# Late weight loads on another queue, sums of the first gate group on VectorE, another PSUM bank, and another order from the scheduler in a hybrid FoX/RWKV-7 layer

## The chip, the cores and the metric

The kernel runs on one core of a Trainium2 chip. The metric is device time in microseconds of one execution. Engines are named as the profile names them: PE is TensorE (matmuls; PEld its weight loads), DVE is VectorE, ACT is ScalarE, POOL is GpSimd, and SP (SPq in a timeline) is SyncE, which here only issues DMAs.

## What is computed

T = 512 tokens of width 2048 go through one layer with two branches. In outline:

```
h = rmsnorm(x) * norm_gain;  u = h @ w_in;  split u -> u_fox, u_rwkv, g_a, g_b
o_a = causal attention with forget gates over q, k, v (8 heads of 128) * silu(z_a)
r, kr, vr, z_b, w_down, a_down = token_shift(u_rwkv)          # 16 heads of 64
decay = exp(-exp(w));  a = sigmoid(a0 + a_down @ a2);  kk = kr*k_k / max(|kr*k_k|, eps)
S = S*decay + (S @ -kk) (kk*a)^T + v k^T;  y = S r           # for every token
o_b = (groupnorm(y) + bonus) * silu(z_b)
m = sigmoid(g_a) * (o_a @ w_proj_fox) + sigmoid(g_b) * (o_b @ w_proj_rwkv)
out = final_rmsnorm(x + m @ w_out)
```

## The kernel before

All products are done in float32 accuracy: each operand is split into a high and a low part, and a product is three matmuls (high by high, high by low, low by high). A weight piece is loaded by SP as `raw_*`, ACT writes its high part `whi_*` (line 267) and DVE its low part `wlo_*` (line 268).

The first stage runs 16 units in turn: `rw0`, `fox0`, ..., `rw7`, `fox7`. A unit is a list of weight products (`u_*`); between their matmuls PE does the small work of the scan and of the attention heads. The scan is done for pairs of heads (p = 0 to 7) in chunks of 64 tokens (c = 0 to 7). Each pair has a front (`rwkv_front`: the norm `kn`, root on ACT at line 537, TENSOR_SCALAR at 538 and four RECIPROCALs at 541 on DVE; the decays `tz`, lines 520 to 523; then `E1`, `EK`, `AR`, `rkk`, `rhi`/`rlo`), a back (`rwkv_back`: `BK` and the matrices of the chunks), and a chain (`rwkv_chain`, lines 696 to 774). The chain goes through the chunks one after the other. For chunk c: the matmul `z` gives a PSUM tile, whose two halves are copied to `zt` by DVE (line 717) and ACT (718); the matmul `sa` reads `zt`, and its result is copied to `AV` by DVE (727) and ACT (728); the matmul `st` reads `AV`; two DVE operations make the next state `SV` from it (735), which the next chunk's `z` reads. In the time of pair p's chain, PE also runs the front of pair p+1.

The order of PE and of SP is the order of the program text, which a planner with fixed lags (`LAG`) interleaves from the workers. The orders of DVE, ACT and POOL are set by the framework's scheduler from what is ready and from priorities: the chain's operations, for one, are written under a high priority (`HP`).

Then come the gates. Stage `c` (lines 1071 to 1102, the columns of one quarter for each group g = 0 to 3) uses weight pieces `g{g}_{kb}_{k}`; its two PSUM tiles `c11_g_0` and `c11_g_1` are of the kind `ps_mm` (two banks), which the units before it use too: `fz` at line 848 reads the last of them. While it runs, DVE makes the sums `d1`, `s3`, `s2` and `s4` of quarters of the activations (`sum_step`). The other quarters are computed by `gates_rest` with fewer products, from sums of weight blocks: for each group units "5" (block 11 + 12), "7" (12 + 22), "6", "3" and "4", each of four steps j of 12 matmuls with weights of 128x1024, whose parts `h` and `l` ACT and DVE split from `X` or `b`. For the first group (g = 0), `X` is loaded, block 12 is added onto it by an accumulating DMA, and so are later 22 (line 994) and 21 (998). These DMAs are issued by POOL for the first four units, and later plain loads by SP. The first group's units 5 and 7 alternate over j, then come the four steps of 6. `open_late` (938) opens the pool of `gates_rest` as soon as all chains have ended. After the gates follow the two projections (`p`) and the output product (`o`), whose first weights are `raw_p0_0_0` to `_3`.

Of the kernel before, what the change touches and what calls it, by code (L numbers as in the profile page):

```python
# [9 lines left out]
F32 = mybir.dt.float32  # L10
F32R = mybir.dt.float32r
AF = mybir.ActivationFunctionType
ALU = mybir.AluOpType
# [4 lines left out]
P = 128  # L18
# [24 lines left out]
HP = 300  # L43
# [13 lines left out]
def hybrid_layer(  # L57
# [6 lines left out]
    nc = tc.nc  # L64
    V, S, G, PE = nc.vector, nc.scalar, nc.gpsimd, nc.tensor
# [76 lines left out]
    def ps_mm(name):  # L142
        return psm.tile([P, T], F32, tag="mm", bufs=2, name=name)

    def ps_ms(name):
        return psm.tile([P, T], F32, tag="ms", bufs=3, name=name)
# [146 lines left out]
    def u_tile(name):  # L293
        ps = ps_mm(f"u_{name}")
        yield from product(ps, name, lambda k: hhi[:, k, :], lambda k: hlo[:, k, :])
        return ps
# [18 lines left out]
    def gate_w(g, kb, cb, j, n=2):  # L315

        c0 = (GB0 if g < 2 else GA0) + g % 2 * 1024 + cb * 512
        r0 = (kb * KB + j * n) * P
        return w_in[r0:r0 + n * P, c0:c0 + 512]
# [24 lines left out]
    for hf in range(2):  # L344
        t = slice(256 * hf, 256 * hf + 256)
# [75 lines left out]
    def split(hi, lo, a):  # L421

        S.copy(hi, a)  # L423
        V.tensor_tensor(lo, a, hi.bitcast(F32), ALU.subtract)  # L424
# [55 lines left out]
    p1_d = dram.tile([4, 2, P, T], F32, name="p1_d")  # L480

    def tt(eng, o, a, b, op=ALU.mult):
        eng.tensor_tensor(o, a, b, op)  # L483
# [375 lines left out]
    def stage1():  # L859
        ps = yield from u_tile("ad")  # L860
# [5 lines left out]
        for kind, i in units:  # L866
            if kind == "rw":
                for nm, blk in (("k", 1), ("r", 0), ("z", 3), ("v", 2)):
                    ps = yield from u_tile(f"{nm}{i}")
# [68 lines left out]
        def open_late():  # L938

            if not opened and chain.done:  # L940
                rw_stack.close()
                opened.append(late_stack.enter_context(tc.tile_pool(name="gw", bufs=1, reuse_waits="tile")))
                rest.append(gates_rest(opened[0]))
                next(rest[0])


        def gates_rest(wp):
# [5 lines left out]
            raw, xs, ready = {}, {}, {}  # L953
            at = [0]

            def load(upto):
                while at[0] < len(loads) and loads[at[0]][0] <= upto:
                    n, b = loads[at[0]]
                    at[0] += 1
                    g, p, j = units[n]  # L960
                    onto = g == 0 and b == "11"
                    if onto:
                        t = xs[j] = wp.tile([P, 2, 512], F32, tag="X", bufs=4, name=f"X_{g}{j}")
                    else:
                        t = wp.tile([P, 2, 512], F32, tag=f"b{b}", bufs=3 if b == "22" else 2, name=f"b{b}_{g}{p}{j}")

                    with tc.high_priority(offset=HP if n < 4 else 0):
                        (G if n < 4 else nc.sync).dma_start(t, rows(g, b, j))
                        if onto:
                            G.dma_start(t, rows(g, "12", j), accum_op=ALU.add)  # L970
                    raw[n, b] = t

            def rows(g, b, j):
                return gate_w(g, int(b[0]) - 1, int(b[1]) - 1, j).rearrange("(k p) m -> p k m", p=P)

            def prep(n):
                g, p, j = units[n]
                if p == "5" and g == 0:
                    src = xs[j]
                elif p == "5":  # L980
                    src = xs[j] = wp.tile([P, 2, 512], F32, tag="X", bufs=4, name=f"X_{g}{j}")
                    tt(V, src, raw[n, "11"], raw[n, "12"], ALU.add)
                elif p == "7":
                    src = raw[n - 1, "12"]
                    tt(V, src, src, raw[n, "22"], ALU.add)
                else:
                    src = raw[n, "22"] if p == "3" else xs[j]
                hi = wp.tile([P, 2, 512], F32R, tag="hi", bufs=3, name=f"h{g}{p}{j}")
                lo = wp.tile([P, 2, 512], F32R, tag="lo", bufs=3, name=f"l{g}{p}{j}")
                split(hi, lo, src)  # L990
                ready[n] = (hi, lo)
                if p == "7":
                    if g == 0:
                        G.dma_start(xs[j], rows(g, "22", j), accum_op=ALU.add)
                    else:
                        tt(V, xs[j], xs[j], raw[n, "22"], ALU.add)
                elif p == "6":
                    G.dma_start(xs[j], rows(g, "21", j), accum_op=ALU.add)

# [5 lines left out]
                    done.append(m)  # L1005

            done = []
            load(1)
            ready_upto(1)
            yield  # L1010
            left = [("s4", j) for j in range(4)]
            ev = lambda tag, nm: wp.tile([P, T], F32, tag=tag, bufs=4 if tag == "p1" else 2, name=nm)
            for n, (g, p, j) in enumerate(units):
                ready_upto(n + 2)
                load(n + 4)
                if (p, j) == ("5", 0):
                    pz = [ps_mm(f"z5_{g}_{t}") for t in range(2)]
                    p1 = [ev("p1", f"p1_{g}_{t}") for t in range(2)]
                    for t in range(2):
                        (G if g == 0 else nc.sync).dma_start(p1[t], p1_d[g, t])  # L1020
                elif (p, j) == ("7", 0):
                    if g % 2:
                        px = [ps_ms(f"x7_{g}"), ps_y(f"y7_{g}")]
                    else:
                        px = [psm.tile([P, T], F32, tag="ch", bufs=2, name=f"x7_{g}_{t}") for t in range(2)]
                elif (p, j) == ("6", 0):
                    py = [ps_ms(f"y6_{g}_{t}") for t in range(2)]
                ps = pz if p in "53" else px if p in "74" else py
                hi, lo = ready.pop(n)
                begin, end = p in "576", p in "634"  # L1030
                for t in range(2):
                    for kk in range(2):
                        k = 2 * j + kk
                        th, kb = {"7": (1, 0), "6": (0, 0), "3": (0, 1), "4": (1, 1)}.get(p, (0, 0))
                        if p == "5":
                            ah, al = (a[:, kk, t * P:(t + 1) * P] for a in d1[j])
                        else:
                            ts = slice(256 * th + t * P, 256 * th + (t + 1) * P)
                            ah, al = (a[:, KB * kb + k, ts] for a in (hhi, hlo))
                        for a, w, i in ((ah, hi, 0), (ah, lo, 1), (al, hi, 2)):  # L1040
                            mm(ps[t], a, w[:, kk, :], start=begin and k == 0 and i == 0,
                               stop=end and k == KB - 1 and i == 2, skip_group_check=True)
                            yield
                    if j < 3:
                        continue
                    if p == "5":
                        p5 = [None, None] if t == 0 else p5
                        p5[t] = ev("p5", f"p5_{g}_{t}")
                        S.copy(p5[t], ps[t])
                    elif p == "6":  # L1050
                        tt(V, p1[t], p1[t], py[t], ALU.add)
                        u3 = ev("u3", f"u3_{g}_{t}")
                        tt(V, u3, p1[t], px[t], ALU.add)
                        tt(V, p5[t], p5[t], u3, ALU.subtract)
                        S.activation(p5[t], p5[t], AF.Tanh, scale=0.5)
                        store_gate(p5[t], g, 1, 1, t)
                    elif p == "3":
                        u3 = ev("u3", f"c12_{g}_{t}")
                        tt(V, u3, pz[t], p1[t], ALU.subtract)
                        S.activation(u3, u3, AF.Tanh, scale=0.5)  # L1060
                        store_gate(u3, g, 0, 1, t)
                    elif p == "4":
                        tt(V, p1[t], p1[t], px[t], ALU.add)
                        S.activation(p1[t], p1[t], AF.Tanh, scale=0.5)
                        store_gate(p1[t], g, 1, 0, t)
                if g == 3 and p in "34" and j % 2 == 0:
                    split_o(len(o_first), 0, ob_d)
                if left and p == "6":
                    sum_step(*left.pop(0))

        rest = []
        for g in range(4):
            ps = [ps_mm(f"c11_{g}_{t}") for t in range(2)]
            for kb in range(2):
                for j in range(4):
                    ws = [next_piece(), next_piece()]
# [3 lines left out]
                    for kk, t in order:  # L1080
# [7 lines left out]
                        if j == 3 and kk == 1:  # L1088
                            if kb == 0:
                                p1 = keep.tile([P, T], F32, tag=KEEP[t], name=f"p1_{g}_{t}")  # L1090
# [9 lines left out]
                        sum_step(*first_sums.pop(0))  # L1100
                    if g == 3 and kb == 1 and not first_sums:
                        sum_step("s2", j)
                    open_late()
        if first_sums or len(d1) < 4:
            raise ValueError("the sums come too late")
        while not opened:
# [96 lines left out]
    for tb in range(4):  # L1203
        t = fin.tile([P, D], F32, tag="xo", bufs=4, name=f"xo_{tb}")
# [98 lines left out]
```

## Time and profile before

| | us |
|---|---|
| median of 3 runs | 1668.12 (1667.06 to 1669.88) |
| the profiled execution | 1671.53 |
| its span in the profile | 1669.8 |
| PE busy | 1603.4 |
| DVE busy | 1118.0 |
| ACT busy | 770.0 |
| POOL busy | 118.3 |

The durations used below come from the one profiled execution. Its time is 3.4 us above the median. Idle time of PE is the span less PE's busy time; the list of waits says for what it was idle, and a timeline gives each instruction's start, its duration and, in brackets, the idle time ahead of it with what ended that.

### The profile page before, as it was taken

The numbers are of one execution on the slowest core, as the hardware profiler recorded it, in microseconds if no ns is written. First come the engines' busy times: TensorE is split into PE (matmuls) and PEld (weight loads), VectorE is DVE, ScalarE is ACT, GpSimd is POOL, SyncE is SP. The second block draws the span as 40 slices with busy tenths as digits, with TensorE's granted clock in tenths as the row PEclk, the third lists the DMA queues.
The fourth block names the chain that finished last, engine by engine and source line by source line (L and its number), as shares of the span: only waits on it lengthen the run. The fifth ranks groups of instructions, "written<-read, shape, count | busy, mean of one in ns | idle before, by whom it ended". The sixth has DMA issues, their size and how long they took to land. (4 is left out here: it accounts for less than half of the span.)

```text
span 1669.8 us, 23495 instructions
## 1 busy us (share of the span) xinstructions
PE 1603.4 (96%) x8378; PEld 1302.3 (78%) x8378; DVE 1118.0 (67%) x2165; ACT 770.0 (46%) x1503; POOL 118.3 (7%) x181
## 2 busy tenths in 40 slices
PE   6999999999999999999999899599999999999998
PEld 6888787787887877877878677478888788888886
DVE  6467777786687777776876779677877335444432
ACT  7533645536446445464464376344445223323322
POOL 3010000000001000001000000311000000001110
PEclk9999999999999999999999999799999999999999
DMA  5343334243333342433333466997776545563422
GB/s 167 98 105 90 84 86 106 61 120 86 86 93 96 90 106 70 111 87 86 90 98 92 117 190 197 261 279 191 237 236 174 163 153 164 158 202 132 139 82 101
DMA packets 239595, 220.58 MB, mean 132 GB/s; under 512 B 40454, under 2 KB 174190, under 8 KB 238838
## 3 DMA queue, kind: packets, MB, share of 16 engines
q1 hardware_dynamic: 222662, 179.73, 38.3%
q0 software_dynamic: 9616, 25.72, 6.6%
q10 hardware_dynamic: 7200, 13.63, 2.2%
q8 instruction: 66, 1.08, 0.3%
q14 instruction: 51, 0.42, 0.1%
HBM read 198.04 MB, written 20.99 MB: 131 GB/s over the span
## 5 line engine op out<-in xcount | busy, mean ns | idle before, releaser
L136 PE MATMUL p<-whi_p,o 128*128 128x512 f32 x512 | 164.3, 398 | 2.3 <-ACT whi_p L267 2.3
L136 PEld LDWEIGHTS p<-whi_p,o 128*128 128x128 f32 x512 | 97.0, 190 | 24.4 <-ACT whi_p L267 2.7
L483 DVE TENSOR_TENSOR Wt<-W,Lt 128x16 f32<-128x16 f32 (+30 forms) x248 | 101.6, 410 | 6.5
L268 DVE TENSOR_TENSOR wlo_p<-raw_p,whi_p 128x512 fp32r<-128x512 f32 x64 | 43.5, 691 | 91.9 <-ACT whi_p L267 91.9
L136 PE MATMUL p<-wlo_p,o 128*128 128x512 f32 x256 | 101.4, 396 | 0.3 <-DVE wlo_p L268 0.2
L267 ACT ACTIVATE whi_p<-raw_p 128x512 fp32r<-128x512 f32 x64 | 40.4, 632 | 119.0 <-PE p L136 47.4
L268 DVE TENSOR_TENSOR wlo_o<-raw_o,whi_o 128x512 fp32r<-128x512 f32 x56 | 42.3, 761 | 69.8 <-ACT whi_o L267 69.5
L136 PE MATMUL o<-whi_o,mhi 128*128 128x512 f32 x224 | 87.6, 391 | 0.0
L136 PE MATMUL o<-whi_o,mlo 128*128 128x512 f32 x224 | 87.2, 389 | 0.0
L136 PE MATMUL o<-wlo_o,mhi 128*128 128x512 f32 x224 | 87.1, 389 | 0.0
L423 ACT CAST h<-X 128x1024 fp32r<-128x1024 f32 x48 | 50.1, 1051 | 79.4 <-DMA X<-in_w_in_dram 22.7
L424 DVE TENSOR_TENSOR l<-X,h 128x1024 fp32r<-128x1024 f32 x48 | 58.4, 1223 | 31.9 <-ACT h L423 31.9
L643 DVE TENSOR_REDUCE W<-Wt 128x8 f32<-128x16 f32 (+30 forms) x248 | 72.7, 293 | 5.7
L267 ACT ACTIVATE whi_o<-raw_o 128x512 fp32r<-128x512 f32 x56 | 35.2, 631 | 78.5 <-PE o L136 70.8
L136 PE MATMUL c<-whi_g,hhi 128*128 128x512 f32 x128 | 52.4, 409 | 7.2 <-DVE fz L848 4.5
L136 PEld LDWEIGHTS p<-wlo_p,o 128*128 128x128 f32 x256 | 48.4, 189 | 11.6 <-DVE wlo_p L268 1.0
L722 ACT ACTIVATE pre<-SV,E 64x64 f32<-64x64 f32 x112 | 38.6, 345 | 39.7 <-DVE SV L735 38.4
L267 ACT ACTIVATE whi_g<-raw_g 128x512 fp32r<-128x512 f32 x64 | 39.9, 630 | 31.6 <-PE c L136 14.3
L268 DVE TENSOR_TENSOR wlo_g<-raw_g,whi_g 128x512 fp32r<-128x512 f32 x64 | 43.2, 686 | 14.2 <-ACT whi_g L267 13.5
L136 PE MATMUL u_fq<-hhi,whi_fq 128*128 128x512 f32 x128 | 52.5, 410 | 0.0
L136 PE MATMUL u_fq<-hlo,whi_fq 128*128 128x512 f32 x128 | 52.4, 409 | 0.0
L136 PE MATMUL c<-wlo_g,hhi 128*128 128x512 f32 x128 | 52.0, 406 | 0.2 <-DVE wlo_g L268 0.2
(428 smaller groups left out, 4671.6 us busy)
## 6 DMA issues: line engine op xcount, KB each, us to landing
b<-in_w_in_dram SPq DMA_DIRECT2D x56, 512.0 KB
raw_g<-in_w_in_dram SPq DMA_DIRECT2D x64, 256.0 KB
raw_o<-in_w_out_dram SPq DMA_DIRECT2D x56, 256.0 KB
X<-in_w_in_dram POOLq DMA_DIRECT2D x26, 512.0 KB, 7.1
raw_k<-in_w_in_dram SPq DMA_DIRECT2D x32, 256.0 KB
raw_r<-in_w_in_dram SPq DMA_DIRECT2D x32, 256.0 KB
raw_z<-in_w_in_dram SPq DMA_DIRECT2D x32, 256.0 KB
raw_v<-in_w_in_dram SPq DMA_DIRECT2D x32, 256.0 KB
```

Of the source, the lines that this page charges most:

```text
L136: PE.matmul(out, lhsT=lhsT, rhs=rhs, start=start, stop=stop, **kw)
L267: S.activation(whi, raw, AF.Copy)
L268: V.tensor_tensor(wlo, raw, whi.bitcast(F32), ALU.subtract)
L423: S.copy(hi, a)
L424: V.tensor_tensor(lo, a, hi.bitcast(F32), ALU.subtract)
L483: eng.tensor_tensor(o, a, b, op)
L643: V.tensor_reduce(W[:, :, i], tmp[:, :, 0:i + 1], AX.X, ALU.add)
L722: S.activation(pre[hs[q]], SV[hs[q], c, q, :], AF.Copy, scale=E1[hs[q], c, CH:CH + 1])
```

## The change

Five things are changed. (1) For g = 0 the blocks 11, 12 and 22 are plain loads by SP like those of the other groups, and DVE adds them: `X` = b11 + b12, and `X` += b22 behind unit 7. (2) The tiles `p1` of g = 0 are loaded by SP, too. (3) The second tile of the first group's `c` sum is in the bank of `ps_y`. (4) `open_late` is called in the last step of `c` only. (5) The framework's scheduler sets the orders of DVE, ACT and POOL by a time line of its own. The orders of PE and SP are as before but for the loads named; on DVE 1409 of 2165 instructions, on ACT 532 of 1499 stand at another place, and POOL has 16 DMAs fewer.

```diff
                     g, p, j = units[n]
-                    onto = g == 0 and b == "11"
-                    if onto:
-                        t = xs[j] = wp.tile([P, 2, 512], F32, tag="X", bufs=4, name=f"X_{g}{j}")
-                    else:
-                        t = wp.tile([P, 2, 512], F32, tag=f"b{b}", bufs=3 if b == "22" else 2, name=f"b{b}_{g}{p}{j}")
-
-                    with tc.high_priority(offset=HP if n < 4 else 0):
-                        (G if n < 4 else nc.sync).dma_start(t, rows(g, b, j))
-                        if onto:
-                            G.dma_start(t, rows(g, "12", j), accum_op=ALU.add)
+                    t = wp.tile([P, 2, 512], F32, tag=f"b{b}", bufs=3 if b == "22" else 2, name=f"b{b}_{g}{p}{j}")
+                    nc.sync.dma_start(t, rows(g, b, j))
...
-                if p == "5" and g == 0:
-                    src = xs[j]
-                elif p == "5":
+                if p == "5":
...
                 if p == "7":
-                    if g == 0:
-                        G.dma_start(xs[j], rows(g, "22", j), accum_op=ALU.add)
-                    else:
-                        tt(V, xs[j], xs[j], raw[n, "22"], ALU.add)
+                    tt(V, xs[j], xs[j], raw[n, "22"], ALU.add)
...
-            load(1)
...
-                        (G if g == 0 else nc.sync).dma_start(p1[t], p1_d[g, t])
+                        nc.sync.dma_start(p1[t], p1_d[g, t])
...
-            ps = [ps_mm(f"c11_{g}_{t}") for t in range(2)]
+            ps = [ps_mm(f"c11_{g}_0"), (ps_mm if g else ps_y)(f"c11_{g}_1")]
...
-                    open_late()
+                    if g == 3 and kb == 1 and j == 3:
+                        open_late()
...
-    with _tile.TileContext(nc) as tc:
+    with _tile.TileContext(nc, schedule_with_timeline_sim=True) as tc:
```

The first place is DVE in chain 2, chunks 1 and 2, where the front of pair 3 is done. In a name the first number is the pair (`_2_`, `_3`), the second the chunk; `kn_3` is the norm of pair 3. Before:

```order
L717 COPY zt_2_4111<-z_2_1_4109 64x64
L727 COPY AV_2_4017<-sa_2_1_4161 64x64
L538 TENSOR_SCALAR kn_3_4143<-kn_3_4143 128x512
L541 RECIPROCAL kn_3_4143<-kn_3_4143 128x128 x2
L735 SCALAR_TENSOR_TENSOR SV_2_3271<-st_2_1_4172,E1_0_483,pre_2_4114 64x64 x2
L268 TENSOR_TENSOR wlo_v3_8_4211<-raw_v3_8_4102,whi_v3_8_4210 128x512
L521 TENSOR_SCALAR tz_3_4127<-tz_3_4127 128x512
L541 RECIPROCAL kn_3_4143<-kn_3_4143 128x128
L717 COPY zt_2_4194<-z_2_2_4192 64x64
L522 SCALAR_TENSOR_TENSOR tz_3_4127<-reset_531,tz_3_4127 128x512
L268 TENSOR_TENSOR wlo_v3_12_4246<-raw_v3_12_4177,whi_v3_12_4245 128x512
L447 SCALAR_TENSOR_TENSOR z_3_4203<-u_z3_4029,par1m_452,z_3_4203 128x511
```

After, from the same `zt` of chunk 1 on:

```order
L717 COPY zt_2_4111<-z_2_1_4109 64x64
L268 TENSOR_TENSOR wlo_v3_4_4180<-raw_v3_4_4080,whi_v3_4_4179 128x512
L538 TENSOR_SCALAR kn_3_4143<-kn_3_4143 128x512
L541 RECIPROCAL kn_3_4143<-kn_3_4143 128x128 x4
L521 TENSOR_SCALAR tz_3_4127<-tz_3_4127 128x512
L727 COPY AV_2_4017<-sa_2_1_4161 64x64
L483 TENSOR_TENSOR EK_3_4132<-EK_3_4132,k_3_3859 128x512
L543 SCALAR_TENSOR_TENSOR kn_3_4143<-k_3_3859,par_448,kn_3_4143 128x512
L522 SCALAR_TENSOR_TENSOR tz_3_4127<-reset_531,tz_3_4127 128x512
L551 SCALAR_TENSOR_TENSOR rkk_3_4155<-r_3_4025,par_448,EK_3_4132 128x512
L735 SCALAR_TENSOR_TENSOR SV_2_3271<-st_2_1_4172,E1_0_483,pre_2_4114 64x64 x2
```

and further, to the copy of chunk 2's `AV`:

```order
L268 TENSOR_TENSOR wlo_v3_8_4211<-raw_v3_8_4102,whi_v3_8_4210 128x512
L546 SCALAR_TENSOR_TENSOR AR_3_4151<-kn_3_4143,E1_1_484 128x8x64
L483 TENSOR_TENSOR AR_3_4151<-r_3_4025,E1_1_484 128x8x64
L483 TENSOR_TENSOR BK_3_4324<-EK_3_4132 64x8x64 x2
L717 COPY zt_2_4194<-z_2_2_4192 64x64
L268 TENSOR_TENSOR wlo_v3_12_4246<-raw_v3_12_4177,whi_v3_12_4245 128x512
L447 SCALAR_TENSOR_TENSOR z_3_4203<-u_z3_4029,par1m_452,z_3_4203 128x511
L424 TENSOR_TENSOR rlo_3_4158<-rkk_3_4155,rhi_3_4157 128x512
L483 TENSOR_TENSOR BK_3_4324<-kn_3_4143,EK_3_4132 64x8x64 x2
L727 COPY AV_2_4017<-sa_2_2_4218 64x64
```

The copy `AV_2` from `sa_2_1` stood ahead of the front's first operation and now stands behind six of them (one TENSOR_SCALAR, four RECIPROCALs and the TENSOR_SCALAR of `tz`); the rest of the front, which was spread up to chunk 3, now stands between `AV` of chunk 1 and `AV` of chunk 2.

The second place is DVE in chain 3, chunks 0 and 1, with the front of pair 4. Before:

```order
L727 COPY AV_3_5208<-sa_3_0_5239 64x64
L268 TENSOR_TENSOR wlo_v4_4_5318<-raw_v4_4_5214,whi_v4_4_5317 128x512
L735 SCALAR_TENSOR_TENSOR SV_3_4387<-st_3_0_5293,E1_1_484,pre_3_5229 64x64 x2
L538 TENSOR_SCALAR kn_4_5275<-kn_4_5275 128x512
L541 RECIPROCAL kn_4_5275<-kn_4_5275 128x128 x2
L717 COPY zt_3_5309<-z_3_1_5307 64x64
L521 TENSOR_SCALAR tz_4_5259<-tz_4_5259 128x512
L541 RECIPROCAL kn_4_5275<-kn_4_5275 128x128
L268 TENSOR_TENSOR wlo_v4_8_5345<-raw_v4_8_5244,whi_v4_8_5344 128x512
L727 COPY AV_3_5208<-sa_3_1_5328 64x64
L522 SCALAR_TENSOR_TENSOR tz_4_5259<-reset_531,tz_4_5259 128x512
L483 TENSOR_TENSOR EK_4_5264<-EK_4_5264,k_4_4990 128x512
```

After:

```order
L727 COPY AV_3_5208<-sa_3_0_5239 64x64
L268 TENSOR_TENSOR wlo_v4_4_5318<-raw_v4_4_5214,whi_v4_4_5317 128x512
L538 TENSOR_SCALAR kn_4_5275<-kn_4_5275 128x512
L541 RECIPROCAL kn_4_5275<-kn_4_5275 128x128 x4
L521 TENSOR_SCALAR tz_4_5259<-tz_4_5259 128x512
L735 SCALAR_TENSOR_TENSOR SV_3_4387<-st_3_0_5293,E1_1_484,pre_3_5229 64x64 x2
L483 TENSOR_TENSOR EK_4_5264<-EK_4_5264,k_4_4990 128x512
L268 TENSOR_TENSOR wlo_v4_8_5345<-raw_v4_8_5244,whi_v4_8_5344 128x512
L543 SCALAR_TENSOR_TENSOR kn_4_5275<-k_4_4990,par_448,kn_4_5275 128x512
L522 SCALAR_TENSOR_TENSOR tz_4_5259<-reset_531,tz_4_5259 128x512
L717 COPY zt_3_5309<-z_3_1_5307 64x64
L551 SCALAR_TENSOR_TENSOR rkk_4_5287<-r_4_5147,par_448,EK_4_5264 128x512
```

Here it is the state `SV_3` of chunk 0 that stood ahead of `kn_4` and now stands behind the TENSOR_SCALAR, the four RECIPROCALs and that of `tz_4`.

The third place is SP's queue behind the first pieces of the projection (`raw_p0`), with the loads of `gates_rest` (b11, b12, b22 of group 0; the last digit is j). Before:

```order
L240 DMA raw_p0_0_3_10713<-in_w_proj_rwkv_dram 128x512
L968 DMA X_02_10755<-in_w_in_dram 128x2x512
L968 DMA b12_052_10758<-in_w_in_dram 128x2x512
L968 DMA b22_072_10784<-in_w_in_dram 128x2x512
L968 DMA X_03_10804<-in_w_in_dram 128x2x512
L968 DMA b12_053_10807<-in_w_in_dram 128x2x512
L968 DMA b22_073_10827<-in_w_in_dram 128x2x512
```

After:

```order
L240 DMA raw_p0_0_3_10692<-in_w_proj_rwkv_dram 128x512
L962 DMA b11_050_10727<-in_w_in_dram 128x2x512
L962 DMA b12_050_10729<-in_w_in_dram 128x2x512
L962 DMA b22_070_10737<-in_w_in_dram 128x2x512
L962 DMA b11_051_10745<-in_w_in_dram 128x2x512
L962 DMA b12_051_10747<-in_w_in_dram 128x2x512
L962 DMA b22_071_10755<-in_w_in_dram 128x2x512
L962 DMA b11_052_10757<-in_w_in_dram 128x2x512
L962 DMA b12_052_10759<-in_w_in_dram 128x2x512
L1006 DMA p1_0_0_10763<-p1_d_561 128x512
L1006 DMA p1_0_1_10764<-p1_d_561 128x512
L962 DMA b22_072_10785<-in_w_in_dram 128x2x512
```

SP got the ten loads that POOL had issued; they stand behind `raw_p0_0_3` as SP's first late load did. On DVE, the split of the first unit now follows a sum of two loads:

```order
L483 TENSOR_TENSOR X_00_10731<-b11_050_10727,b12_050_10729 128x1024
L483 TENSOR_TENSOR st_s4_1_10964<-hhi_99 128x512
L424 TENSOR_TENSOR hlo_100<-st_s4_0_10938,hhi_99 128x2x256
L483 TENSOR_TENSOR b12_050_10729<-b12_050_10729,b22_070_10737 128x1024
L424 TENSOR_TENSOR l050_10734<-X_00_10731,h050_10733 128x1024
L483 TENSOR_TENSOR su_s4_1_10965<-hlo_100 128x512
L483 TENSOR_TENSOR X_01_10749<-b11_051_10745,b12_051_10747 128x1024
L424 TENSOR_TENSOR l070_10741<-b12_050_10729,h070_10740 128x1024
L483 TENSOR_TENSOR X_00_10731<-X_00_10731,b22_070_10737 128x1024
```

Eight such sums are new on DVE: four of b11 and b12, and four that add b22 to `X`. Before, `X` came ready from the accumulating DMA.

## Rows read from the trace of the kernel before

**Rows 1.** The page: span, then part 1, busy time and share of each engine.
```profile
span 1669.8 us, 23495 instructions
...
PE 1603.4 (96%) x8378; PEld 1302.3 (78%) x8378; DVE 1118.0 (67%) x2165; ACT 770.0 (46%) x1503; POOL 118.3 (7%) x181
```

**Rows 2.** PE's waits: line waited for, total us, times, longest.
```profile
PE z L136 <- ACT h L423: 18.5, 3, 14.4
...
PE c L136 <- DVE fz L848: 4.5, 1, 4.5
```

**Rows 3.** Timeline of PE at the end of c: start, us, line, names, idle.
```profile
1063.98 0.79 PE L136 MATMUL z<-h,d_fqh 128*128 128x512 f32 x1 [14.38 <-ACT h L423]
```

**Rows 4.** Chain of work that ended last: start us, us, what.
```profile
1100.15 10.99 PE y L136 x48
```

**Rows 5.** Windows: stretch, us, busy time of each engine, clock, DMA.
```profile
45.00:950.00 905.00, 888.10 (x5077) 720.47 (x5075) 674.89 (x1518) 452.66 (x975) 46.55 (x61) 1.00 0.37 93
```

**Rows 6.** Timeline of DVE, chain 2 with the front of pair 3.
```profile
407.27 0.22 DVE L727 COPY AV<-sa 64x64 f32<-64x64 f32 x1 [1.68 <-PE sa L136]
407.77 0.43 DVE L538 TENSOR_SCALAR kn<-kn 128x512 f32<-128x512 f32 x1 [0.28 <-ACT kn L537]
408.24 1.76 DVE L541 RECIPROCAL kn<-kn 128x128 f32<-128x128 f32 x2
409.92 0.48 DVE L735 SCALAR_TENSOR_TENSOR SV<-st,E,pre 64x64 f32<-64x64 f32 x2
410.53 0.69 DVE L268 TENSOR_TENSOR wlo_v<-raw_v,whi_v 128x512 fp32r<-128x512 f32 x1
411.13 0.42 DVE L521 TENSOR_SCALAR tz<-tz 128x512 f32<-128x512 f32 x1
...
412.59 1.21 DVE L522 TENSOR_TENSOR_SCAN tz<-reset,tz 128x512 f32<-128x512 bf16 x1
...
417.68 0.75 DVE L543 SCALAR_TENSOR_TENSOR kn<-k,par,kn 128x512 f32<-128x512 f32 x1
```

**Rows 7.** Timeline of ACT at the same place.
```profile
405.85 1.28 ACT L537 ACT_TABLE_LOAD   x1
407.14 0.60 ACT L537 ACTIVATE kn<-kn 128x512 f32<-128x512 f32 x1
```

**Rows 8.** Timeline of PE at the same place.
```profile
408.75 0.38 PE L136 MATMUL st<-AV,BT 128*128 128x128 f32 x2
...
415.46 0.49 PE L136 MATMUL st<-AV,BT 128*128 128x128 f32 x2
...
419.31 0.39 PE L136 MATMUL z<-SV,G 128*128 128x128 f32 x2
```

**Rows 9.** Timeline of ACT, chain 3 with the front of pair 4.
```profile
517.60 0.60 ACT L537 ACTIVATE kn<-kn 128x512 f32<-128x512 f32 x1
```

**Rows 10.** Timeline of PE, chain 3.
```profile
520.54 0.39 PE L136 MATMUL z<-SV,G 128*128 128x128 f32 x2
...
526.70 0.39 PE L136 MATMUL z<-SV,G 128*128 128x128 f32 x2
```

**Rows 11.** Windows, the stretch behind PE's wait for fz.
```profile
937.00:940.50 3.50, 3.50 (x10) 2.71 (x9) 2.61 (x7) 1.26 (x2) 0.00 (x0) 0.51 0.36 101
```

**Rows 12.** Timeline of PE in the c stage, behind a shorter idle time.
```profile
961.51 0.50 PE L136 MATMUL c<-whi_g,hhi 128*128 128x512 f32 x1 [2.36 <-ACT whi_g L267]
```

**Rows 13.** The page, part 5: all wlo_g operations.
```profile
L268 DVE TENSOR_TENSOR wlo_g<-raw_g,whi_g 128x512 fp32r<-128x512 f32 x64 | 43.2, 686 | 14.2 <-ACT whi_g L267 13.5
```

**Rows 14.** Timeline of SP's queue ahead of the late loads.
```profile
1042.35 4.87 SPq L240 DMA_DIRECT2D raw_p<-in_w_proj_rwkv_dram  x4
```

**Rows 15.** DMA issues, 1035 to 1100 us: count, KB each, median us to landing.
```profile
X<-in_w_in_dram POOLq DMA_DIRECT2D x11, 512.0 KB, 8.1
```

**Rows 16.** DVE's groups by form, 1095 to 1250 us: busy us, mean ns.
```profile
L424 DVE TENSOR_TENSOR l<-X,h 128x1024 fp32r<-128x1024 f32 x35 | 42.6, 1222 | 16.8 <-ACT h L423 16.8
...
L483 DVE TENSOR_TENSOR X<-b,b 128x1024 f32<-128x1024 f32 x11 | 13.5, 1223 | 5.2 <-DMA b<-in_w_in_dram 5.1
```


## The prediction

> **What bounds the kernel now.** I first read the busy shares of the page: TensorE (PE) works 96% of the span [rows 1], so time can be won only from its 66.4 us of idle (1669.8 less 1603.4) and from stretches at a low clock, and every new wait of PE is paid in full, since PE's order is the same after the change. Next the list of PE's waits [rows 2]: the largest is for ScalarE's `h` (14.4 us at once), then 4.5 us for `fz`. The timeline shows the place of the first [rows 3]: the first `z` matmul stands at 1063.98 after 14.38 us of idle, so the `c` stage ended at 1049.6. In the chain of work that ended last, unit 6 starts at 1100.15, and its 48 matmuls take 10.99 us [rows 4]. The eight units between, 96 matmuls, need 22.0 us at that pace and took 50.55, so 28.5 us are lost there. From 45 to 950 us, where the scan's chain, its fronts and the weight products interleave, PE idles only 905 - 888.1 = 16.9 us, `fz` included [rows 5]. So two things are to be weighed: what the change gives back of 28.5 and 4.5 us, and whether the new orders of VectorE (DVE) and ScalarE (ACT) keep up with a PE that had almost no gap.
>
> **Part A: the new order puts the next pair's front ahead of the chain.** In each pair but the first, the chain of the earlier pair (z, `zt`, sa, `AV`, st, `SV`) meets the front of the next (norm of `kn`: root on ACT, one TENSOR_SCALAR and four RECIPROCALs on DVE; then `tz`, `EK`, `AR`, `BK`). Before, `AV` of chunk 1 is copied at 407.27, ahead of the front, and the RECIPROCALs come in pieces between chain items [rows 6]. After, it stands behind the TENSOR_SCALAR, all four RECIPROCALs and the TENSOR_SCALAR of `tz`, and the rest of the front is as tightly packed between the next items. DVE can't run ahead of that: the TENSOR_SCALAR waits for ACT's root (407.14 + 0.60), which follows a table load (405.85 + 1.28) [rows 7] behind ACT's copy of `zt`, and ACT's order there is the same.
>
> The sum for chain 2: from 407.77 DVE has no gap up to `AV` of chunk 2. Start to start, a TENSOR_SCALAR of `kn` takes 0.47 (407.77 to 408.24), a RECIPROCAL 0.84 (two from 408.24 to 409.92), the one of `tz` 0.34, the scan 1.13 (its 1.21 less the overlap), a 128x512 operation 0.62 (410.53 to 411.13 is 0.60, the scalar forms take a little more), a small copy 0.14, the pair of `SV` 0.5 [rows 6]. `AV` of chunk 1 is done at 407.77 + 0.47 + 4 x 0.84 + 0.34 + 0.2 = 412.1; its user st stood at 408.75 [rows 8], so PE waits 3.4 us. Up to `AV` of chunk 2 there are 13 operations of 128x512 (EK, kn, rkk, two AR, four BK, two wlo, z, rlo): 0.47 + 3.36 + 0.34 + 1.13 + 13 x 0.62 + 0.9 for the small ones = 14.3, so it ends at 422.05. The st that uses it stood at 415.46 [rows 8]: PE is 6.6 us late there, in four waits (st 3.4, then z, sa, st about 1 each). DVE is by then through with the front, and the next z has 3.85 us behind st (419.31 less 415.46), so the lag ends.
>
> Chain 3 is of the other kind: `SV` of chunk 0 stands behind the block. Its front can begin when ACT's root ends, 517.60 + 0.60 [rows 9]. The same sum (two pairs of `SV`, 13 large operations) is 518.25 + 0.47 + 3.36 + 0.34 + 1.13 + 8.06 + 1.3 = 532.9 for `SV` of chunk 1, whose z stood at 526.70: 6.2 us. The first of its waits is 2.5 us (`SV` of chunk 0 at 523.0, z before at 520.54) [rows 10].
> The order shows chains 4 and 6 built like 2, 5 like 3, and 1 with as much ahead of `zt` and `AV`, where I take 6; chains 0 and 7 hardly change. A = 3 x 6.6 + 2 x 6.2 + 6 = **+38 us**. If only the first wait of each block counts, it is 3 x 3.4 + 2 x 2.5 + 2.3 = 17.5; an upper end is 45, one more 1 us wait in each, for a weight's `wlo` behind the block.
>
> ACT's copy of the same `AV` also stands later, behind a table load and four instructions (1.28 and some 2.6 us): done at about 411.8, a little before DVE's, it adds nothing. The root starts 0.01 us behind its table load [rows 7]. The Trainium skill, "ScalarE: Activation LUTs", section "What ACT_TABLE_LOAD costs", gives 1283 ns for the load and a drain of 1380 ns with it; the load agrees with the row, no drain is seen in it. By the page ACT's copy would be the later one and A, by an estimate from it, 6 x 1.1 = 6.6 us larger: 1702 instead of 1695, inside the range.
>
> **Part B: the clock.** After the 4.5 us wait for `fz` PE ran 3.5 us at a granted clock of 0.51, the 1.2 GHz level [rows 11], which costs about 1.7 us; after 2.36 us of idle at 961.51 the matmuls are of full-clock length again at once [rows 12]. No 3.4 us wait is in the trace. By the nearest rows I let three of the six first waits cost it: **+5 us**, from 0 (none) to 10 (all).
>
> **Part C: another bank for the first `c` sum.** Its second half no longer waits for `fz` to leave a bank of ps_mm; ps_y's is free there. The 4.5 us and their half-rate stretch go: **-6.2 us**; -3 if `whi_g` or `wlo_g` is next late.
>
> **Part D: the `c` stage.** DVE's order now puts ten sum operations ahead of the last `wlo_g`: 10 x 0.61 (start to start of a 0.69 us operation) = 6.1 us. DVE idles 14.2 us ahead of the 64 `wlo_g` [rows 13], so part of it hides: **+2.5**, from 0 to 5.
>
> **Part E: loads by SyncE (SP), sums by DVE.** Before, Pool issues `X`, then an accumulating DMA onto it, and each j moves 2.5 MB, b12 and b22 being read twice. After, it is 1.5 MB in plain loads, but they stand on SP behind `raw_p` 0 to 3, whose issue runs from 1042.35 for 4.87 us [rows 14]: the first goes out at 1047.2, only 2.4 us before `c` ends. Two loads are needed for the first sum; with 8.1 us each from issue to landing [rows 15], side by side, it starts at about 1056. From there DVE does 19 operations of 128x1024 at 1.22 [rows 16] (4 X, 4 b, 8 `l`, 3 X += b22) and 11 of 128x512 at 0.61: 23.2 + 6.7 = 29.9. So the last `l` of unit 7 comes at 1086, its 12 matmuls end at 1087 to 1089 instead of 1100.15: **-13 us**; -6 if the loads land late, -20 if SP gets ahead of its row. Pool's work taken away is on no path once DVE adds.
> The later opening of the pool (only in the last `c` step) costs nothing, since no load could be issued before SP is at it. Everything behind 1100 keeps its order: 0, with 3 us to either side.
>
> **How the numbers follow.** 38 + 5 - 6.2 + 2.5 - 13 = +26.5. Against the profiled execution's 1671.5 that is 1698; the median of the runs is 3.4 below that execution, so **1695** for it. Chance 0.58.
>
> **Rivals.** (1) Only the first wait of each block counts, since PE's lateness itself gives DVE the time to clear the front: 17.5 - 6.2 + 2.5 - 13 with B at 0 is +0.8, so **1669**, not slower; with E at -20 it is 1662. It decides if the waits that follow each first one stay under about 0.2 us. For it: DVE's busy share is 67% [rows 1]. Against it: the row sum, in which DVE has no gap for 14 us. 0.16 (of it 0.09 faster, 0.06 same, 0.01 slower).
> (2) The transition is hidden whole, 28.5 won instead of 13: **1680**. This needs the first loads some 7 us earlier than SP's row shows. 0.09.
> (3) The loads and DVE's 19 wide operations cost as much as the accumulating DMAs, so that the change doesn't bring its data earlier, E = 0: **1708**. For it, SP's late place. 0.09.
> (4) The clock falls twice in every block: 12 half-rate stretches x 1.7 = 20 for B's 5, **1710**. The row after the 4.5 us wait [rows 11] speaks for it, the 2.36 us one [rows 12] against it. 0.08. The Trainium skill, "TensorE: Matmul & The Clock Gate", section "What's actually happening", has a clock that is throttled by default and released by activity; by it waits that follow each other would weigh more than one alone, which no row here shows.
>
> **The range** takes in the rivals but the far side of (1): **1673 to 1711**. Differences within 0.2% (3.3 us) are about what can't be told from no change: faster 0.09, same 0.06, slower 0.85.
>
> **What would show it.** In the trace after, PE's waits for `AV`, `SV` and `zt` of the chain go from some 6 us to about 35, in six places of up to four waits, with `AV` done some 4.5 us behind the root's end. The wait of `c` for `fz` is gone. The wait ahead of the first `z` is some 8 us, and unit 6 starts 37 to 39 us after the end of `c`. Wrong would be: chain waits of 1 us or less at the fronts (A falls, and the forecast with it); no idle ahead of the first `z` (rival 2); half-rate stretches at every front (rival 4).

## The result and the profile after

| | before | after |
|---|---|---|
| median of the runs | 1668.49 us (4 runs) | 1708.07 us (4 runs, 1707.63 to 1709.52) |
| ratio, 95% interval | | 1.0239 (1.0221 to 1.0256) |
| profiled execution, its span | 1671.53, 1669.8 | 1708.25, 1706.5 |

The changed kernel is 39.6 us slower by the medians. The profiled executions differ by 36.7 us, since that of before stood 3.0 us above its median; the trace explains the 36.7. PE's busy time rose by 12.4 us for the same 8378 matmuls, its idle time by 24.3 (the first lines of the page):

```profile
span 1706.5 us, 23499 instructions
...
PE 1615.8 (95%) x8378; PEld 1306.0 (77%) x8378; DVE 1132.7 (66%) x2173; ACT 775.1 (45%) x1503; POOL 96.4 (6%) x165
```

In the list of PE's waits the chain now leads, where [rows 2] had `h` and `fz`. Columns: what PE waited for, us in total, times, longest. First the chain's three lines before, then the list after.

```profile
PE sa L136 <- ACT zt L718: 4.3, 7, 1.1
PE st L136 <- ACT AV L728: 1.3, 4, 0.8
PE z L136 <- DVE SV L735: 0.3, 1, 0.3
```

```profile
PE sa L136 <- ACT zt L718: 17.9, 16, 4.0
PE st L136 <- ACT AV L728: 17.0, 12, 2.9
PE z L136 <- DVE SV L735: 9.8, 7, 2.7
...
PE z L136 <- ACT h L423: 5.2, 1, 5.2
```

The chain's three come to 44.7 us, against 5.9 before. The wait for `fz` is gone.

Since PE's order is the same in all kernels of this study, each matmul can be looked up in two traces, and the difference of its starts says how late PE is by then. Summed by stretches (all times in the trace of before; "idle" is the change of PE's idle time, "rest" is what the matmuls took longer):

| stretch of before, us | what is there | change | idle | rest |
|---|---|---|---|---|
| 280-330 | chain 1, front 2 | +6.6 | +4.3 | +2.3 |
| 400-425 | chain 2, front 3 | +9.9 | +7.0 | +2.9 |
| 505-545 | chain 3, front 4 | +7.6 | +5.6 | +2.0 |
| 620-645 | chain 4, front 5 | +6.8 | +5.1 | +1.7 |
| 735-770 | chain 5, front 6 | +7.9 | +5.9 | +2.0 |
| 850-885 | chain 6, front 7 | +8.9 | +6.1 | +2.8 |
| the rest up to 925 | front 1 (+2.7), ahead of chain 2 (+2.3), others | +4.4 | | |
| 925-945 | the wait for `fz` | -6.4 | -4.5 | -1.9 |
| 945 to the end of `c` | stage `c` | +6.8 | | |
| end of `c` to unit 6 | transition | -14.5 | | |
| behind it | | -1.3 | | |

The six fronts hold 47.7 us, 34.0 of them idle and 13.7 in matmuls that took longer, most of it at a lower clock. Chain 2 as an example, PE's timeline (start, us, line, names, idle ahead of it and what ended it); the same four matmuls stood at 408.75, 411.30, 413.31 and 415.46 before, without a wait (the first and the last are in [rows 8]):

```profile
422.17 0.49 PE L136 MATMUL st<-AV,BT 128*128 128x128 f32 x2 [2.91 <-ACT AV L728]
...
425.57 0.46 PE L136 MATMUL z<-SV,G 128*128 128x128 f32 x2 [0.62 <-DVE SV L735]
...
430.26 0.43 PE L136 MATMUL sa<-zt,DT 128*128 128x64 f32 x2 [2.61 <-ACT zt L718]
...
434.21 0.80 PE L136 MATMUL st<-AV,BT 128*128 128x128 f32 x2 [0.95 <-ACT AV L728]
```

And DVE there, to be read beside [rows 6]: `AV` comes behind the TENSOR_SCALAR, the four RECIPROCALs in one piece and `tz`, and from 417.30 to 433.50 DVE has no gap.

```profile
417.30 0.43 DVE L538 TENSOR_SCALAR kn<-kn 128x512 f32<-128x512 f32 x1 [1.46 <-ACT kn L537]
417.76 3.39 DVE L541 RECIPROCAL kn<-kn 128x128 f32<-128x128 f32 x4
421.07 0.69 DVE L521 TENSOR_SCALAR tz<-tz 128x512 f32<-128x512 f32 x1
421.68 0.20 DVE L727 COPY AV<-sa 64x64 f32<-64x64 f32 x1
...
427.27 2.46 DVE L483 TENSOR_TENSOR BK<-EK 64x512 f32<-64x512 f32 x2
429.75 0.22 DVE L717 COPY zt<-z 64x64 f32<-64x64 f32 x1
...
433.28 0.22 DVE L727 COPY AV<-sa 64x64 f32<-64x64 f32 x1
```

The list names ACT's copy as the last releaser, but ACT's copy of `AV` started at 421.91 behind 0.70 us of waiting for DVE's. The lower clock, in windows laid on the slow stretches of the fronts (columns: stretch, length, busy time of PE, PEld, DVE, ACT, POOL, then granted clock, DMA share, GB/s):

```profile
300.40:304.90 4.50, 4.50 (x12) 3.31 (x12) 4.50 (x8) 1.98 (x4) 0.76 (x1) 0.50 0.06 10
...
431.10:438.20 7.10, 6.15 (x18) 4.32 (x17) 3.61 (x8) 2.27 (x8) 0.00 (x0) 0.52 0.17 38
543.60:546.70 3.10, 3.08 (x9) 1.91 (x8) 3.07 (x6) 0.68 (x2) 0.00 (x0) 0.54 0.29 76
664.00:666.90 2.90, 2.90 (x9) 2.32 (x9) 2.90 (x5) 0.62 (x2) 0.00 (x0) 0.53 0.35 90
783.70:786.20 2.50, 2.50 (x8) 2.02 (x8) 2.50 (x4) 0.18 (x1) 0.00 (x0) 0.50 0.25 50
912.60:920.10 7.50, 6.94 (x20) 4.86 (x19) 3.36 (x7) 2.30 (x8) 0.00 (x0) 0.55 0.28 70
```

Every front has one, at the 1.2 GHz level; before, none had. They are 27.6 us long together; PE is busy in 26.1 us of them, and half of that, 13.0 us, is all but 0.7 us of the fronts' "rest". Where the clock falls differs. In chains 1, 3, 4 and 5 it falls in or just behind the front's first wait (3.96, 2.65, 2.41 and 2.65 us), with no other wait of over 0.3 us in the 15 us ahead of it. In chains 2 and 6 it is still at full speed behind the first two waits and falls behind the third. The first waits of chains 4 and 6 are almost equal, and the `st` behind them takes 0.80 us in one and 0.49 in the other:

```profile
663.54 0.80 PE L136 MATMUL st<-AV,BT 128*128 128x128 f32 x2 [2.41 <-ACT AV L728]
```

```profile
903.41 0.49 PE L136 MATMUL st<-AV,BT 128*128 128x128 f32 x2 [2.42 <-ACT AV L728]
```

The transition: `c` ends at 1107.29 - 5.23 = 1102.06 and the first matmul of unit 6 starts at 1138.00, 35.9 us later; before it was 50.4 (the same matmul at 1099.99, and the end of `c` by [rows 3]). Of the 14.5 us, 9.2 come from the wait ahead of the first `z`, 1.6 from waits behind it, and 3.7 from matmuls that took less time. In stage `c` there is one new wait of weight, 2.23 us for ACT's copy of `p1`:

```profile
1090.01 0.80 PE L136 MATMUL c<-whi_g,hhi 128*128 128x512 f32 x1 [2.23 <-ACT p L1078]
...
1107.29 0.80 PE L136 MATMUL z<-h,d_fqh 128*128 128x512 f32 x1 [5.23 <-ACT h L423]
...
1138.00 0.39 PE L136 MATMUL y<-h,hhi 128*128 128x512 f32 x1
```

### The profile page after: what moved, and what is told of

Read it like the earlier page. It is cut to its first block, busy times and chain, and to the rows that moved or that the text cites. A ratio compares the mean times of both kernels' runs of the same rounds, so it can differ in the third digit from the quotient of the medians.

```text
span 1706.5 us, 23499 instructions
## 1 busy us (share of the span) xinstructions
PE 1615.8 (95%) x8378; PEld 1306.0 (77%) x8378; DVE 1132.7 (66%) x2173; ACT 775.1 (45%) x1503; POOL 96.4 (6%) x165
## 3 DMA queue, kind: packets, MB, share of 16 engines
q1 hardware_dynamic: 224582, 183.40, 38.2%
## 4 chain that ended last, share of the span: by engine, by line
PE 75%; DVE 12%; DMA 5%; ACT 4%; issue 3%; SPq 2%; ACTq 0%; DVEq 0%; POOL 0%
PE o L136 10%; PE p L136 10%; PE z L136 5%; PE u_v L136 5%; PE u_k L136 4%; PE y L136 4%; PE u_fk L136 4%; PE u_fq L136 4%; PE u_r L136 4%; PE u_fv L136 4%; PE u_fz L136 4%; PE x L136 3%; PE u_z L136 3%; PE c L136 3%; DVE kn L541 1%
## 5 line engine op out<-in xcount | busy, mean ns | idle before, releaser
L423 ACT CAST h<-X 128x1024 fp32r<-128x1024 f32 x48 | 50.4, 1052 | 58.7 <-DVE X L483 21.1
L423 ACT CAST h<-b 128x1024 fp32r<-128x1024 f32 x32 | 33.7, 1052 | 49.5 <-PE y L136 24.6
L136 PE MATMUL u_z<-hhi,whi_z 128*128 128x512 f32 x128 | 53.8, 421 | 0.0
L136 PE MATMUL u_z<-hhi,wlo_z 128*128 128x512 f32 x128 | 53.8, 420 | 0.0
L136 PE MATMUL u_z<-hlo,whi_z 128*128 128x512 f32 x128 | 53.6, 419 | 0.0
```

Of the source, the lines that this page charges most:

```text
L136: PE.matmul(out, lhsT=lhsT, rhs=rhs, start=start, stop=stop, **kw)
```

## Experiments

**The change without the scheduler's time line** (e1_own_order):

```diff
-    with _tile.TileContext(nc, schedule_with_timeline_sim=True) as tc:
+    with _tile.TileContext(nc) as tc:
```

> All of the change but the scheduler's time line: the loads by SP, the adds by DVE, the bank and the late opening stay, DVE, ACT and POOL get the order of before up to the gates. Theory (the new order of DVE and ACT makes all the loss): the waits in the chain go back to 6 us and the half-rate stretches at the fronts vanish, the bank (6.4) and the transition (13.4) stay won: 1668.5 - 6.4 - 13.4 = 1649 us (1645 to 1653). Rival (the quick transition of the changed kernel comes from the new order too, not from the plain loads): only the bank is left, 1662 us. Rival (DVE's adds disturb other work): above 1668.

Measured: 1659.1 us against 1670.35 of before on that chip, ratio 0.9937 (0.9913 to 0.9962). The fronts are back to what they were: none of the six differs from before by more than 0.3 us, the list of waits has

```profile
PE sa L136 <- ACT zt L718: 5.0, 8, 1.1
```

and no front has a half-rate stretch. So the order that the time line gives DVE, ACT and POOL makes the whole loss, and the loads give their gain without it: from the end of `c` to unit 6 it is 36.6 us. But 11 us were won, not 20: 3.8 us are lost again from 945 us to the end of `c`, and 2.4 in the gates behind unit 6. Of the bank's 5.8 us, PE's timeline shows where most went:

```profile
943.94 0.50 PE L136 MATMUL c<-wlo_g,hhi 128*128 128x512 f32 x1 [1.30 <-DVE wlo_g L268]
...
947.67 0.50 PE L136 MATMUL c<-whi_g,hhi 128*128 128x512 f32 x1 [1.61 <-ACT p L1078]
...
959.78 0.57 PE L136 MATMUL c<-whi_g,hhi 128*128 128x512 f32 x1 [2.15 <-ACT whi_g L267]
```

The first two stood there with no wait before (the third had 2.36, [rows 12], but now a half-rate stretch follows it).

**The scheduler's time line alone, on the kernel before** (e2_order_alone):

```diff
-    with _tile.TileContext(nc) as tc:
+    with _tile.TileContext(nc, schedule_with_timeline_sim=True) as tc:
```

> The kernel before with the scheduler's time line and nothing else. Theory: the six fronts cost what they cost in the changed kernel, 34.0 us of idle and 13.7 us at the low clock, and some 3 us in between, with neither the bank nor the transition won: 1668.5 + 51 = 1719 us (1713 to 1726). Rival (the order hurts only together with the moved loads, since SP's queue is fuller): within 1 per cent of before, 1660 to 1685.

Measured: 1728.51 us, ratio 1.0352 (1.033 to 1.0374), 58.2 us more. The fronts cost what they cost in the changed kernel (46.1 us in the six), and the chain's waits read the same:

```profile
PE sa L136 <- ACT zt L718: 18.9, 16, 4.0
PE st L136 <- ACT AV L728: 16.4, 12, 2.9
```

The other 12 us are mainly at front 1 (+4.2), ahead of chain 2 (+2.2) and, not expected, from 945 us to unit 6: +4.8 in stage `c`, and +2.5 from its end to unit 6, where PE waits 16.2 us for the first `z` (14.4 before). The two halves add up to 58.2 - 11.2 = 47.0 us and not to 39.6. The profiled executions show most of this difference between 945 us and unit 6: the loss in stage `c` comes with either half (3.8 and 4.8) and doesn't add up (6.8 in the changed kernel), and with the new loads the 2.5 us don't arise.

**The changed kernel without the four RECIPROCALs** (e3_no_reciprocals), to tell DVE's part from ACT's:

```diff
-        V.tensor_scalar(t3, t3, L2_EPS, None, ALU.max)
-        for q4 in range(RS):
+        V.tensor_scalar(t3, t3, L2_EPS, 0.1, ALU.max, ALU.min)
+        for q4 in range(0):
```

> The changed kernel without the four RECIPROCALs of each front (the norm is not inverted, so the scan's input is another); the order around them is all but the same. Theory (VectorE's block ahead of AV and SV sets the waits): each block is 3.4 us shorter, and of 34.0 us idle in the six fronts some 14 stay; with fewer half-rate stretches the time is 1680 to 1690 us. Rival (ScalarE's order alone holds AV: table load, tz, a, EK and a weight split stand ahead of its copy as well): ACT's copy ends only 0.7 us earlier, where AV is the item, and the idle stays above 26 us: 1698 to 1705 us.

Measured: 1699.13 us, ratio to before 1.0173 (1.0144 to 1.0201). The idle time added in the six fronts fell from 34.0 to 26.3 us only; what their matmuls took longer fell from 13.7 to 5.0, since four of the six have no half-rate stretch here. The rival's numbers came out, not mine: 3.4 us of DVE work per front were taken away, and 1.3 us of idle per front. Chain 2 shows why. First DVE, then ACT's copy, then PE:

```profile
416.61 0.43 DVE L538 TENSOR_SCALAR kn<-kn 128x512 f32<-128x512 f32 x1 [1.46 <-ACT kn L537]
...
418.61 0.43 DVE L521 TENSOR_SCALAR tz<-tz 128x512 f32<-128x512 f32 x1 [0.79 <-ACT tz L520]
418.95 0.21 DVE L727 COPY AV<-sa 64x64 f32<-64x64 f32 x1
```

```profile
420.03 0.21 ACT L728 COPY AV<-sa 64x64 f32<-64x64 f32 x1
```

```profile
420.29 0.49 PE L136 MATMUL st<-AV,BT 128*128 128x128 f32 x2 [1.73 <-ACT AV L728]
...
427.33 0.43 PE L136 MATMUL sa<-zt,DT 128*128 128x64 f32 x2 [2.43 <-ACT zt L718]
```

With the RECIPROCALs gone DVE waits for ACT's `tz`, which stands ahead of `AV` on DVE, and then ACT's own copy is last, behind its `tz`, `a` and `EK`. So a wait for `AV` has two orders behind it: DVE's is the later by a little, ACT's stands next. ACT's own idle time in the changed kernel says by how much: of the 27.5 us that PE waits for `AV` and `zt` in the six fronts, ACT's copies had stood 8.7 us for DVE's. The waits for `SV`, 9.8 us, all end with DVE's write. In chain 2 the waits that follow the first (2.43 for `zt`, 2.61 with the RECIPROCALs) hardly get shorter, since the rest of the front is as tightly packed as it was.

**The first unit's loads ahead of `raw_p`** (e4_first_loads_sooner), on e1_own_order:

```diff
-                    if g == 3 and kb == 1 and j == 3:
+                    if g == 3 and kb == 1 and j == 1:
                         open_late()
```

> As e1_own_order, and the loads of the first unit stand on SP ahead of the four raw_p loads instead of behind them (the pool is opened two steps of the c stage earlier). Theory (the first sum waits for SP's late place): 3 to 5 us faster than e1_own_order, 1644 to 1646. Rival (DVE's row of sums and splits sets the end of the transition, whenever the first load lands): within 1 us of e1_own_order.

Measured: 1658.54 us, ratio to before 0.9933 (0.9909 to 0.9957): the same as e1_own_order, as the rival had it. SP issued the loads at 1040.04, 6.4 us sooner; the first sum came 1.5 us sooner, at 1053.56, directly behind a row of `s2` sums in which DVE has no wait for a DMA:

```profile
1052.22 0.69 DVE L483 TENSOR_TENSOR su_s<-d_fpT,hlo 128x512 f32<-128x512 f32 x1
1052.95 0.69 DVE L483 TENSOR_TENSOR st_s<-st_s,su_s 128x512 f32<-128x512 f32 x1
1053.56 1.22 DVE L483 TENSOR_TENSOR X<-b,b 128x1024 f32<-128x1024 f32 x1
```

In this order DVE's sums set the start of the transition, not SP's late place.

**The bank alone** (e5_bank_alone):

```diff
-            ps = [ps_mm(f"c11_{g}_{t}") for t in range(2)]
+            ps = [ps_mm(f"c11_{g}_0"), (ps_mm if g else ps_y)(f"c11_{g}_1")]
```

> The kernel before with the first c sum's second half in the other bank, nothing else. The prediction (part C): 6.2 us less. Theory now, from the first stage c of e1_own_order: the 4.5 us wait and its half-rate stretch go (5.8 us), but wlo_g (1.30), the copy of p1 (1.61) and a new half-rate stretch take some 3.5 to 4 us back within 35 us, since DVE and ACT had caught up in that wait: 1.5 to 2.5 us less than before.

Measured: 1666.89 us, ratio 0.9994 (0.9983 to 1.0005): no difference that can be told, 1.2 us by the medians. In the trace the 925 to 945 stretch is 5.7 us shorter, and the next 30 us are 3.0 us longer (the `wlo_g` wait of 1.29 and that for `p1` of 1.61 are both there); 1.2 us more are given back in the gates. So much of the theory of a gain given back shows. The traces by themselves don't show that all of it comes back: the two profiled executions differ by 5.7 us, since that of before stood 3.4 us above its median and this one 1.1 below.

**Loads, adds and late opening alone** (e6_loads_alone; the change without the time line and without the bank):

```diff
-            ps = [ps_mm(f"c11_{g}_0"), (ps_mm if g else ps_y)(f"c11_{g}_1")]
+            ps = [ps_mm(f"c11_{g}_{t}") for t in range(2)]
```

> The loads by SP, the adds by DVE and the late opening, with the bank and the order of before. The prediction (part E): 13 us less, all in the 50 us behind the end of c. Theory now: 13 us are won there, and some 3 us come back later (a wait for hlo in the first unit 3, and small ones behind it): 9 to 11 us less than before. Rival (bank and loads need each other, since c's end sets the start of the loads): under 6 us less.

Measured: 1658.58 us, ratio 0.9944 (0.9932 to 0.9956), 9.5 us less. From 1020 to unit 6 13.7 us are won, and 2.3 come back behind it. So nearly all that the change wins in e1_own_order (11.2 us, on another chip) is in the loads, the adds and the late opening, which were not run apart.

**The four RECIPROCALs in one piece, on the kernel before** (e7_four_reciprocals_together):

```diff
-        S.activation(t3, psk, AF.Sqrt)
-        V.tensor_scalar(t3, t3, L2_EPS, None, ALU.max)
-        for q4 in range(RS):
-            sl = slice(q4 * T // RS, (q4 + 1) * T // RS)
-            V.reciprocal(t3[:, sl], t3[:, sl])
+        with tc.high_priority(offset=700 if p else 0):
+            S.activation(t3, psk, AF.Sqrt)
+            V.tensor_scalar(t3, t3, L2_EPS, None, ALU.max)
+            for q4 in range(RS):
+                sl = slice(q4 * T // RS, (q4 + 1) * T // RS)
+                V.reciprocal(t3[:, sl], t3[:, sl])
```

> The kernel before with the TENSOR_SCALAR and all four RECIPROCALs of each front in one piece (its own scheduler, a higher priority for them); they stand behind AV of chunk 1 (or SV of chunk 0 in the other kind) and ahead of the next SV (or zt), two more RECIPROCALs than before. By the row sum: 2 x 0.84 us of work against 0.8 to 0.9 us of slack, so 0.8 us of wait in each of six blocks, no half-rate stretch: 5 us slower, 1672 to 1675. Rival (PE's matmuls between hide it): within 1 us of before. Rival (each new wait also costs a half-rate stretch): 12 us or more.

Measured: 1676.26 us, ratio 1.0047 (1.0034 to 1.006), 8.1 us more. The six fronts are 1.4, 1.4, 1.2, 0.7, 1.6 and 1.1 us longer, 7.4 in all, where the row sum gave 5; 1.6 us are won at front 1. The time is just above the 1672 to 1675 expected. In chain 2 `SV` stands behind the whole piece, and PE's z waits 0.71 us for it, as worked out; a second wait of 0.62 for a `zt` further on was not in the sum.

```profile
406.77 0.43 DVE L539 TENSOR_SCALAR kn<-kn 128x512 f32<-128x512 f32 x1 [0.28 <-ACT kn L538]
407.23 3.39 DVE L542 RECIPROCAL kn<-kn 128x128 f32<-128x128 f32 x4
410.54 0.48 DVE L736 SCALAR_TENSOR_TENSOR SV<-st,E,pre 64x64 f32<-64x64 f32 x2
```

```profile
411.16 0.46 PE L136 MATMUL z<-SV,G 128*128 128x128 f32 x2 [0.71 <-DVE SV L736]
...
421.67 0.43 PE L136 MATMUL sa<-zt,DT 128*128 128x64 f32 x2 [0.62 <-ACT zt L719]
```

No front has a half-rate stretch here. The way of summing rows is thus tested on a smaller dose: the price of a few operations ahead of the chain is read from DVE's starts within 1 or 2 us per front, and comes out a little low.

**First units with a high priority** (e8_first_unit_ahead), on e4_first_loads_sooner:

```diff
             def prep(n):
...
+                with tc.high_priority(offset=HP if n < 8 else 0):
```

> As e4_first_loads_sooner, with a high priority for the sums and splits of units 5 and 7 of the first group: they stand ahead of two wlo_p and of the s4 sums on DVE, but still behind the s2 sums. Theory (DVE's row of s2 sums holds the first X): the first z comes some 1 to 2 us sooner than in e4, and the time is 1 to 3 us below e4. Rival (the s2 sums hold all of it): the same as e4 within 1 us.

Measured: 1656.93 us, ratio to before 0.993 (0.9917 to 0.9942), 1.6 us below e4_first_loads_sooner by the medians of different chips, which can't be told apart. PE still waits 8.4 us ahead of the first z, as in e4_first_loads_sooner, which speaks for the rival. It is the fastest of the kernels run, with e4_first_loads_sooner and e1_own_order beside it: all three keep the loads, the adds and the bank without the scheduler's time line, and beat both the kernel before and the changed one.

## Why the prediction was right, and where its sum was not

The forecast was slower, 1695 us, and 1708.1 lies in its range; the place and the mechanism are those that it named. But the sum was 26.5 us against a measured 36.7 between the profiled executions, so some terms were mis-sized. (The printed terms add up to 26.3; with A unrounded, 38.2, they give 26.5. And rival 1, at 1669, lies below the range that was meant to take it in but for its far side.) The measured time is 3 us below the range's upper end. Parts B and D came out above their own bounds, and that the range held is in part luck: A, E and the stretch behind unit 6 gave back 6.8 us of what B, D and the terms put at zero cost more.

- **Part A, 38 us: 34.0.** Chain 2's waits (2.91, 0.62, 2.61, 0.95) are 7.1 for 6.6, chain 3 has 5.6 for 6.2, chain 1 4.3 for 6. `AV` of chunk 1 ended 4.58 us behind the front's start, forecast 4.3. In the account of the cause one thing was missing: e3_no_reciprocals shows that ACT's copy is next in line, which the prediction dismissed as "adds nothing". It adds nothing to the sum, but it means that mending DVE's order alone would win only a part: at chain 2's first `AV` 0.7 of the 2.91 us.
- **Part B, 5 us: 13.7.** This is the step that failed. I let three of six fronts drop the clock once, at most all six (10 us), by the rows of two single waits [rows 11, rows 12]. All six drop it, and three of them stay at half rate for longer (4.5, 7.1 and 7.5 us, against 2.5 to 3.1). Four drop it at the first wait, the place that was priced, and two only behind their third, which was not. Half-rate stretches at every front were named as a sign of being wrong, and the sign came: rival 4's 1710 is nearer to 1708.1 than the forecast's 1695. Its two stretches for each front are borne out at most by those three, and its 20 us were 13.7.
- **Part C, -6.2: -6.4** at its place. What the prediction lacked is that the wait had let DVE and ACT catch up: alone, the bank is worth nothing that can be measured (e5_bank_alone). In the changed kernel nothing is lost from 945 to 975 us (0.5 us are won), where e5_bank_alone lost 3.0; the loss stands further on, in part D.
- **Part D, 2.5: 6.8**, above its bound of 5. It was costed by `wlo_g` alone, and `wlo_g` waits are 1.1 us in all. The larger ones are 2.23 us for ACT's copy of `p1`, which in the new order stands behind a table load and the activation of line 771, and the half-rate stretch behind it; ACT's order in stage `c` wasn't costed.
- **Part E, -13: -14.5.** Confirmed with both orders (36.6 us in e1_own_order, 35.9 in the changed kernel, forecast 37 to 39), and by e6_loads_alone. The wait ahead of the first z was 5.2 us in one piece, forecast 8. Of its working, the bound by SP's place fell: in the old order it is DVE's sums (e4_first_loads_sooner).
- **Put at zero: +4.4 up to 925 us.** Front 1 with chain 0 costs 2.7, though I had read it as hardly changed; ahead of chain 2 a wait of 2.3 us for ACT's `BT` and a half-rate stretch behind it cost 2.3.

Rival 1 (only the first wait counts) is out: the waits behind the first are 4.2 of 7.1 us in chain 2. Rivals 2 and 3 are out by part E.

What stays open: why waits that are nearly alike drop the clock in one place and not in another. The first waits of chains 4 and 6 (2.41 and 2.42 us) differ in this, and chain 2's first, 2.91 us, doesn't drop it. In e3_no_reciprocals chain 2 has waits of 1.73, 2.43 and 1.41 and no half-rate stretch; in the changed kernel 2.91, 0.62 and 2.61, and a stretch of 7.1 us behind the third. In stage `c` the same wait at 961.51 (2.36 before, 2.15 in e1_own_order) has one only in e1_own_order. The length of one wait doesn't decide it. Which part of the loss is due to DVE's order and which to ACT's or POOL's was not separated further than e3_no_reciprocals and ACT's idle time do; none of these orders was run alone.

## What to carry to other kernels

When a scheduler writes a new order, look at each in-order engine for what now stands ahead of a serial chain's small copies, and sum that work from the starts in the old trace: here it gave 38 us where 34.0 came. Add the clock for every place with such new waits, not only for the longest: here waits of 2.0 to 4.0 us dropped it in each of the six fronts, though not every such wait did. And a wait that is taken away is worth only what the engines behind it have in hand: of the 5.7 us that went with the wait for `fz`, 3.0 came back within 30 us as waits for ACT and DVE (e5_bank_alone).

## What the runs showed of the hardware that I had not expected

**VectorE beside GpSimd.** In the new order one of the two `BK<-EK` of each front runs on DVE behind the start of POOL's product `kn` (POOL's timeline in chain 2 of the changed kernel), and takes 1.70 to 1.78 us; the other takes 0.68 or 0.69. So the mean of 1219 ns below mixes two kinds. The groups of the kernel before and of the changed one, 45 to 960 us (count, busy us, mean ns):

```profile
426.92 1.56 POOL L483 TENSOR_TENSOR kn<-kn,a 128x512 f32<-128x512 f32 x1 [5.45 <-DVE AR L546]
```

```profile
L483 DVE TENSOR_TENSOR BK<-EK 64x512 f32<-64x512 f32 x16 | 10.9, 683 | 0.2
```

```profile
L483 DVE TENSOR_TENSOR BK<-EK 64x512 f32<-64x512 f32 x16 | 19.5, 1219 | 0.1
```

That is (19.5 - 10.9) / 8 = 1.1 us per front, in chain 2 between `SV` and `zt`. The Trainium skill, "SBUF — State Buffer", section "Who interferes with whom", says that a DVE instruction with two SBUF inputs contends with a GpSimd instruction that reads SBUF. The traces agree in that every slow `BK<-EK` overlaps POOL's product: in e7_four_reciprocals_together it does in three of the six fronts (1.75 and 1.76 us) and does not in the other three (0.67 and 0.68). But the overlap alone doesn't make DVE slow. Twice in the kernel before, DVE's also starts 0.4 us behind POOL's, and there it took 0.67 or 0.68 us and POOL's product 2.24. One of the two:

```profile
530.69 2.24 POOL L483 TENSOR_TENSOR kn<-kn,a 128x512 f32<-128x512 f32 x1 [5.09 <-DVE AR L546]
```

```profile
531.10 0.67 DVE L483 TENSOR_TENSOR BK<-EK 64x512 f32<-64x512 f32 x1
```

That the 1.1 us make a good part of what the wait of 2.61 us for `zt` has over the forecast of about 1 is argued, not shown.

**The clock** falls in every front of the new order although only one wait there is above 3 us (3.96): 27.6 us at the 1.2 GHz level in six fronts, against none in the six of the kernel before, and none in those of e7_four_reciprocals_together, whose waits are 1.6 us at most.

**Copies of two halves by two engines.** In the traces of this program ACT's copy of `AV` or `zt` always starts behind the end of DVE's copy of the other half (0.70 us of waiting at 421.91), so the last releaser in the list is ACT also where DVE is late. Whether the chip or the program's own synchronization asks for this was not tested.
